# A two-layer hybrid backbone step on one core: substitution columns dealt in turn, R1 made by TensorE, a 3 + 2 split of token tiles behind a norm, and four tiles for the first merge's gates

## The chip, the cores and the metric

The program runs on one core of one Trainium2 chip. The time is that of one execution on the device in microseconds. TensorE (PE) multiplies, VectorE (DVE), ScalarE (ACT) and GpSimd (POOL) work on elements, SyncE (SP) issues all DMAs. TensorE's full clock is 2.4 GHz, its low one 1.2 GHz.

## The reference

Two layers (DEPTH 2) act on 128 context tokens and 512 latent tokens of width 1024, all in float32. A layer projects the modulated input once into three branches (gated MLP over chunks, grouped attention, a bidirectional delta rule), projects each branch back, gates and sums the three, projects the sum, adds it to the input and normalises; then comes an MLP with squared ReLU of width 4096 and a second norm.

```python
f = _token_shift(concat([rkv, lora[:, :, d]]), mu, reverse=(d == 1))       # d = 0, 1
S = S * w_t[:, :, None, :] + sa[..., None] * b_t[:, :, None, :] + v_t[..., None] * k_t[:, :, None, :]
p = einsum('bljc,jcd->bljd', branches, P['w_branch'][l])
mixed = sum(gates * p, axis=2) @ P['w_out'][l]
x = _layer_norm(ALPHA * x + g1 * mixed, ln1_g, ln1_b)
f = square(relu(h @ P['w_up'][l])) @ P['w_down'][l]
x = _layer_norm(ALPHA * x + g2 * f, ln2_g, ln2_b)
```

## The kernel before, in words

The 640 tokens lie as five tiles of 128 (tile 0 is context). Every large product takes weights and inputs split into a high part and a rest (`whalf`, `split`: ScalarE copies the high part, VectorE subtracts, L241 and L242), and three matmuls for each. The instructions are written out in an order by hand; a planner then puts them on the engines' queues by that order as priority, as their inputs and buffers become free in its own timeline, so later work (the gate projections `gl`, say) fills TensorE in earlier stages.

**The delta rule.** There are eight units a layer (four head pairs, two directions). A unit has seven steps: 1, load r, k and the decay; 2, scale them and store the key norms (`ssd`); 3, products G of 64-token chunks and their transposes `bk`; 4, the solve; 5, transposes `av`, products `w`, and the load of the solved blocks into `Ga`; 6, products `z1`, `z2`, `tx`, `xp`; 7, a scan over the chunks in eight steps (`st`). `rwkv` (L647) interleaves them: for each unit u step 3 of u, step 1 of u+1, the solve of u, steps 6 and 7 of u-1, step 5 of u, step 2 of u+1, with pieces of projections and attention between.

**The solve (step 4).** For 40 blocks of 32x32 (two halves, 20 chunk-heads) T = inverse of a unit triangular matrix is made by substitution. The blocks are read from DRAM (`ad` to `ab`) three times, on 120 partitions: group g holds columns 11g to 11g+10 of each block. Each of the 31 steps multiplies (L861) and adds (L862) on all 11 columns of every group; unit 3 of each layer does so on GpSimd, the others on VectorE. Then a copy `Tr` (L864), three writes of `td`, three writes of a transposed `tr`; `td` is loaded into the diagonal blocks of `Ga`, `tr` into `R1`, the operand of z1.

**PSUM.** Pool B has two buffers and serves step 2 (`ss`, `bo`), 3, 5 and 6 of all units. Pool A has two pairs for the projections.

**Behind a norm.** `res_end` normalises tile by tile, transposes a tile and writes its high part and rest into hT (`put_hT`; its last split is L392). `fm_blocks` then does its first three blocks in two parts of the token columns: all three on columns below `CUT` (256: two tiles), then all three on the rest. That is so at three places: the first MLP chunk of either layer, and the second layer's first projection.

**The last of four MLP chunks** starts with rows for the gate and norm, and for each token tile two GpSimd multiplies (L1207) and two VectorE adds of ALPHA x (L1208), ahead of the chunk's first block.

**Merge A** takes, for each of eight output blocks, the gate from DRAM into a tile `f` (two buffers, shared with the gate projections and the branch loads), multiplies the block by it (L1037) and stores the product (`part`). Merge B and C follow; C loads its branches into e0 to e2. e0 to e4 are otherwise a unit's inputs, one buffer each.

Of the kernel before, what the change touches and what calls it, by code (L numbers as in the profile page):

```python
# [40 lines left out]
RS, AFW = (), 512  # L41
FILL, FILLA, NG, CUT = 1, 4, 24, 256
K13 = ["e0", "e1", "e2", "e3", "e4", "w", "w", "Ld", "ec", "bon", "bon", "Y0", "Y1"]
# [15 lines left out]
class Net:  # L59
# [654 lines left out]
    def unit(self, l, hp, d):  # L714
# [134 lines left out]
        nc.vector.tensor_tensor(out=Am, in0=Am, in1=n2.unsqueeze(1).to_broadcast([3 * NB, 32, 32]), op=ALU.mult)  # L849
        nc.gpsimd.memset(raw[:, 0:1024:33], 1.0)  # L850
        T = self.S([3 * NB, CG, 32], "T", bufs=2)
# [5 lines left out]
        for q in range(31):  # L857
            i, js = (q, slice(q + 1, 32)) if d == 0 else (31 - q, slice(0, 31 - q))
            sh = [3 * NB, CG, 31 - q]
            p = Pm[:, :, 0:31 - q]  # L860
            eng.tensor_tensor(out=p, in0=T[:, :, i:i + 1].to_broadcast(sh), in1=Am[:, i, js].unsqueeze(1).to_broadcast(sh), op=ALU.mult)  # L861
            eng.tensor_tensor(out=T[:, :, js], in0=T[:, :, js], in1=p, op=ALU.add)  # L862
        Tr = self.S([3 * NB, 32, CG], "Pm", bufs=2)
        nc.vector.tensor_copy(Tr, T.rearrange("p c i -> p i c"))  # L864
        td = self.dram.tile([2, NI, 32, 32], F32, name=self.nm("td"))
        tr = self.dram.tile([NI, 32, 32], F32, name=self.nm("tr"))
        tdv = td.rearrange("f i s t -> (f i) s t")
        for g in range(3):
            w = min(CG, 32 - CG * g)
            self.load(tdv[:, CG * g:CG * g + w, :], T[g * NB:g * NB + NB, 0:w, :])  # L870
            p0 = g * NB + d * NI
            self.load(tr[:, :, CG * g:CG * g + w], Tr[p0:p0 + NI, :, 0:w])
        yield
# [35 lines left out]
        Z = R1  # L909
        self.load(R1[fa], tr.rearrange("i t s -> t i s"))  # L910
        ps = self.B("z1")
# [114 lines left out]
    def gated(self, l, j, dp, xs):  # L1026

        nc, a = self.nc, self.a
        wb = self.wsplit(a["wbr"][l, j, dp].rearrange("p t k c -> p (t k c)"))
        gs = []  # L1030
        for dt in range(2):
            g = self.K("f" if j == 0 else "fQ"[dt] if j == 1 else "PQ"[dt])
            self.load(g[:, 0:NTOK], self.gate[l][8 * j + 2 * dp + dt])
            ps = self.A("br", None if j else 0)
            self.mm_fm(ps, wb[dt:dt + 1], xs)
            for o, p in self.ev(ps, g):
                nc.vector.scalar_tensor_tensor(o, o, 1.0, p, ALU.add, ALU.mult)  # L1037
            gs.append(g[:, 0:NTOK])
        return gs
# [152 lines left out]
    def mlp(self, l, hT, xsrc, xdst, nxt, side):  # L1192
# [4 lines left out]
        for pc in range(NPC):  # L1197
# [5 lines left out]
            if pc == NPC - 1:  # L1203
                self.res_rows(r, xsrc)
                for t in range(NT):
                    for x, yh, h in self.res_x(r, t):
                        nc.gpsimd.tensor_tensor(out=yh, in0=yh, in1=r.g[0 if t == 0 else 1][h], op=ALU.mult)  # L1207
                        nc.vector.scalar_tensor_tensor(yh, x, ALPHA, yh, ALU.mult, ALU.add)  # L1208
            ups = self.fm_blocks([a["wup"][l, 8 * pc + i].rearrange("p k c -> p (k c)") for i in range(8)], hT, pc == 0)
            for i, ps in enumerate(ups):  # L1210
# [5 lines left out]
                self.split(f, hi, lo)  # L1216
                xs.append((hi, lo))
                self.steps(side, 3)
            if pc == NPC - 1:
# [231 lines left out]
def shape_constants():  # L1451
# [15 lines left out]
    for g in range(3):  # L1467
        for j in range(CG):
            if CG * g + j < 32:
                e[g, :, j, CG * g + j] = 1  # L1470
    o["E"] = e.reshape(6 * NI, CG, 32)
# [40 lines left out]
```

## Time and profile before

| | us |
|---|---|
| three runs | 2956.73, 2965.16, 2951.77 (median 2956.73) |
| profiled execution | 2957.33 |
| its span, first to last instruction | 2955.5 |
| TensorE's mean granted clock | 0.961 of full |

In the rows, PE is a TensorE matmul and PEld its weight load. "out<-in" are the program's names of tiles; "128x512 f32" is partitions x elements. A group's row ends with the mean ns of one instruction, the idle time of the engine ahead of the group, and what ended it. Matmuls overlap, so the ns of one matmul is longer than the distance to the next.

### The profile page before, as it was taken

Reading aid. Unit: us, or ns where it says so; the run is one execution under the profiler, and the core shown is the slowest. Engines: PE = TensorE matmul, PEld = TensorE weight load, DVE = VectorE, ACT = ScalarE, POOL = GpSimd, SP = SyncE. Lnnn points to the kernel's source line nnn. Section 1 sums busy time; section 2 is a strip of 40 time slices with the busy share of each in tenths; the row PEclk is TensorE's granted clock in tenths of the full one; section 3 lists DMA queues with packets and bytes.
Section 4 is the critical chain, followed back from the end, with each engine's and each line's share of the span. In section 5 each row is a group of like instructions: output and inputs, shape, how many; then the busy total and the mean of one; then the engine's idle time right before and its main releaser. Section 6 shows DMA issues by size and latency. Waiting matters only on the chain.

```text
span 2955.5 us, 56368 instructions
## 1 busy us (share of the span) xinstructions
PE 2769.2 (94%) x21248; PEld 2518.1 (85%) x21248; DVE 1957.2 (66%) x3824; ACT 1365.6 (46%) x3206; POOL 681.6 (23%) x869
## 2 busy tenths in 40 slices
PE   7989989999979899999989899899999898999998
PEld 5979877787869889999989788787877798999998
DVE  5686877877777776777464878877676566223346
ACT  3445665565653433232444456654655434342332
POOL 4241271312333400002040312813121014000021
PEclk8989989999989999999999899899999999999999
DMA  8534323343476254545235333333433652222242
GB/s 265 182 113 117 103 84 92 99 112 91 125 241 211 98 150 152 153 147 183 94 107 161 110 112 100 102 86 91 111 93 111 214 172 76 76 76 72 76 134 84
DMA packets 326647, 367.88 MB, mean 124 GB/s; under 512 B 157599, under 2 KB 179607, under 8 KB 326375
## 3 DMA queue, kind: packets, MB, share of 16 engines
q1 hardware_dynamic: 326375, 364.28, 40.9%
q8 instruction: 167, 2.74, 0.4%
q14 instruction: 105, 0.86, 0.1%
HBM read 301.59 MB, written 62.59 MB: 123 GB/s over the span
## 4 chain that ended last, share of the span: by engine, by line
PE 62%; DVE 16%; DMA 10%; ACT 5%; issue 4%; SPq 2%; POOL 1%; DVEq 0%; ACTq 0%; POOLq 0%
PE fm L163 17%; PE tm L207 17%; PE gl L163 7%; PE br L163 4%; PE tm L233 2%; SPq L125 2%; PE uA L163 2%; PE g L820 2%; DVE T L862 2%; DVE Pm L861 2%; PE xp L939 1%; DVE lo L242 1%; PE st L974 1%; DMA ab<-ad 1%; PE ada L319 1%
## 5 line engine op out<-in xcount | busy, mean ns | idle before, releaser
L242 DVE TENSOR_TENSOR lo<-raw,hi 128x512 fp32r<-128x512 f32 x514 | 381.9, 745 | 402.2 <-ACT hi L241 391.2
L163 PE MATMUL fm<-h,hi 128*128 128x320 f32 (+1 forms) x2720 | 616.5, 316 | 14.8 <-ACT h L391 10.2
L241 ACT ACTIVATE hi<-raw 128x512 fp32r<-128x512 f32 x514 | 323.0, 630 | 593.6 <-PE tm L207 320.2
L163 PEld LDWEIGHTS fm<-h,hi 128*128 128x128 f32 x2720 | 464.5, 192 | 33.0 <-ACT h L391 11.5
L163 PE MATMUL fm<-h,lo 128*128 128x320 f32 (+2 forms) x1360 | 421.7, 316 | 8.4 <-DVE lo L242 8.3
L163 PE MATMUL gl<-h,hi 128*128 128x320 f32 x1536 | 375.6, 322 | 0.0
L163 PEld LDWEIGHTS gl<-h,hi 128*128 128x128 f32 x1536 | 263.4, 191 | 19.5 <-issue 10.7
L163 PEld LDWEIGHTS fm<-h,lo 128*128 128x128 f32 x1360 | 259.8, 192 | 12.9 <-DVE lo L242 9.6
L163 PE MATMUL gl<-h,lo 128*128 128x320 f32 x768 | 248.2, 324 | 1.9 <-DVE lo L242 1.9
L861 DVE TENSOR_TENSOR Pm<-T,ab 120x341 f32<-120x341 f32 (+30 forms) x434 | 171.7, 396 | 9.0
L862 DVE TENSOR_TENSOR T<-T,Pm 120x341 f32<-120x341 f32 (+30 forms) x434 | 170.3, 392 | 9.5
L312 DVE SCALAR_TENSOR_TENSOR acc<-P,c_sg,acc 128x512 f32<-128x512 f32 x196 | 143.3, 771 | 45.6 <-DMA P<-in_wada_dram 44.9
L1207 POOL TENSOR_TENSOR X<-X,e 128x512 f32<-128x512 f32 x8 | 11.6, 1456 | 682.5 <-DMA e<-modd 354.6
L207 PE MATMUL tm<-hi,h 128*128 128x256 f32 x800 | 158.7, 292 | 0.0
L163 PEld LDWEIGHTS gl<-h,lo 128*128 128x128 f32 x768 | 146.8, 191 | 9.0 <-issue 2.5
L163 PE MATMUL br<-h,hi 128*128 128x320 f32 x512 | 123.1, 329 | 23.1 <-DVE f L1037 11.8
L207 PEld LDWEIGHTS tm<-hi,h 128*128 128x128 f32 x800 | 129.2, 195 | 4.8 <-issue 1.6
L207 PE MATMUL tm<-hi,L 128*128 128x256 f32 x720 | 131.8, 283 | 0.0
L978 ACT ACTIVATE q1k<-st,edge 64x64 f32<-64x64 f32 x320 | 98.2, 307 | 66.1 <-PE st L974 60.5
L537 POOL TENSOR_TENSOR P<-P,Q 128x512 f32<-128x512 f32 x64 | 83.6, 1307 | 154.6 <-ACT Q L532 53.2
L207 PE MATMUL tm<-lo,h 128*128 128x256 f32 x400 | 115.9, 291 | 3.1 <-DVE lo L242 3.1
L163 PEld LDWEIGHTS br<-h,hi 128*128 128x128 f32 x512 | 89.4, 198 | 29.6 <-DVE f L1037 9.4
(560 smaller groups left out, 6879.2 us busy)
## 6 DMA issues: line engine op xcount, KB each, us to landing
raw<-in_win_f_dram SPq DMA_DIRECT2D x172, 256.0 KB
raw<-in_wup_dram SPq DMA_DIRECT2D x128, 256.0 KB
raw<-in_wdn_dram SPq DMA_DIRECT2D x128, 256.0 KB
P<-in_wada_dram SPq DMA_DIRECT2D x114, 256.0 KB
w<-rk SPq DMA_DIRECT2D x48, 321.5 KB
gate<-f SPq DMA_DIRECT2D x48, 320.0 KB
raw<-in_wbr_dram SPq DMA_DIRECT2D x48, 256.0 KB
Ld<-rk SPq DMA_DIRECT2D x64, 160.0 KB
```

Source lines behind the costliest of these rows:

```text
L125: self.nc.sync.dma_start(out=out, in_=in_)
L163: nc.tensor.matmul(ps.at(h), w[:, c], ps.of(h, x), start=(k == 0 and p == 0), stop=(k == n - 1 and p == 2))
L207: nc.tensor.matmul(out[t], x[:, ts], w[:, c], start=(k == 0 and p == 0 and (alone or t < 2)), stop=(k == n - 1 and p == 2 and (alone or t ...
L233: nc.tensor.matmul(o, x[:, ts], w[:, c], start=(k == 0 and p == 0), stop=(k == n - 1 and p == 2))
L241: self.nc.scalar.activation(hi, x, AF.Copy)
L242: self.nc.vector.tensor_sub(lo, x, hi.bitcast(F32))
L312: nc.vector.scalar_tensor_tensor(acc[:, s], w, cs[:, k, s:s + 1], acc[:, s], ALU.mult, ALU.add)
L537: nc.gpsimd.tensor_tensor(out=den, in0=den, in1=PT, op=ALU.add)
L820: nc.tensor.matmul(pg[h][:, 128 * j:128 * j + 128], BK[pr, c0 + j].rearrange("p s t -> p (s t)"), RAV[pr, c0 + j, 0:2, :].rearrange("p s t ...
L861: eng.tensor_tensor(out=p, in0=T[:, :, i:i + 1].to_broadcast(sh), in1=Am[:, i, js].unsqueeze(1).to_broadcast(sh), op=ALU.mult)
L862: eng.tensor_tensor(out=T[:, :, js], in0=T[:, :, js], in1=p, op=ALU.add)
L978: nc.scalar.activation(St[kr, s, h, :], p4[kr, s, h, :], AF.Copy, scale=edge[kr, cc:cc + 1])
```

## The change

Columns are dealt: group g now holds columns g, g+3, g+6 and so on of each block, and step q works only on the columns that can be non-zero by then (q//3 + 1 of 11). The memset of the diagonal, the copy `Tr` and the DRAM tensor `tr` are gone; `td` is written column by column. R1 is made in step 6 by matmuls of `Ga`'s diagonal blocks with the identity, into two tiles of pool B, and a ScalarE copy of each. CUT is 384 (three tiles, then two). Merge A's gates go to e0 to e3 in turn. In the last MLP chunk tile i's multiplies and adds stand behind block i.

```diff
--- before.py
+++ after.py
@@ -39,7 +39,7 @@
 EARLY = 2
 ADAR, FIRST = (12, 3), 5
 RS, AFW = (), 512
-FILL, FILLA, NG, CUT = 1, 4, 24, 256
+FILL, FILLA, NG, CUT = 1, 4, 24, 384
 K13 = ["e0", "e1", "e2", "e3", "e4", "w", "w", "Ld", "ec", "bon", "bon", "Y0", "Y1"]
 RAWB, WB = 3, 3
 
@@ -847,7 +847,6 @@
         nc.vector.reciprocal(n2, n2)
         Am = raw.rearrange("p (s t) -> p s t", s=32)
         nc.vector.tensor_tensor(out=Am, in0=Am, in1=n2.unsqueeze(1).to_broadcast([3 * NB, 32, 32]), op=ALU.mult)
-        nc.gpsimd.memset(raw[:, 0:1024:33], 1.0)
         T = self.S([3 * NB, CG, 32], "T", bufs=2)
         Pm = self.S([3 * NB, CG, 32], "Pm", bufs=2)
         nc.vector.tensor_tensor(out=T, in0=c["E"], in1=n2.unsqueeze(1).to_broadcast([3 * NB, CG, 32]), op=ALU.mult)
@@ -856,20 +855,15 @@
         eng = nc.gpsimd if on_pool else nc.vector
         for q in range(31):
             i, js = (q, slice(q + 1, 32)) if d == 0 else (31 - q, slice(0, 31 - q))
-            sh = [3 * NB, CG, 31 - q]
-            p = Pm[:, :, 0:31 - q]
-            eng.tensor_tensor(out=p, in0=T[:, :, i:i + 1].to_broadcast(sh), in1=Am[:, i, js].unsqueeze(1).to_broadcast(sh), op=ALU.mult)
-            eng.tensor_tensor(out=T[:, :, js], in0=T[:, :, js], in1=p, op=ALU.add)
-        Tr = self.S([3 * NB, 32, CG], "Pm", bufs=2)
-        nc.vector.tensor_copy(Tr, T.rearrange("p c i -> p i c"))
+            cs = slice(0, q // 3 + 1) if d == 0 else slice(max(0, (31 - q) // 3), CG)
+            sh = [3 * NB, cs.stop - cs.start, 31 - q]
+            p = Pm[:, cs, 0:31 - q]
+            eng.tensor_tensor(out=p, in0=T[:, cs, i:i + 1].to_broadcast(sh), in1=Am[:, i, js].unsqueeze(1).to_broadcast(sh), op=ALU.mult)
+            eng.tensor_tensor(out=T[:, cs, js], in0=T[:, cs, js], in1=p, op=ALU.add)
         td = self.dram.tile([2, NI, 32, 32], F32, name=self.nm("td"))
-        tr = self.dram.tile([NI, 32, 32], F32, name=self.nm("tr"))
         tdv = td.rearrange("f i s t -> (f i) s t")
         for g in range(3):
-            w = min(CG, 32 - CG * g)
-            self.load(tdv[:, CG * g:CG * g + w, :], T[g * NB:g * NB + NB, 0:w, :])
-            p0 = g * NB + d * NI
-            self.load(tr[:, :, CG * g:CG * g + w], Tr[p0:p0 + NI, :, 0:w])
+            self.load(tdv[:, g::3, :], T[g * NB:g * NB + NB, 0:(34 - g) // 3, :])
         yield
         X = self.units["X"] = self.units.get("X") or self.big1("X", [128, NI, 128])
         X4 = X.rearrange("p (c h) n -> p c h n", h=2)
@@ -907,7 +901,12 @@
         ra, rb_ = ([slice(64 * h + o, 64 * h + o + 32) for h in range(2)] for o in (a_, b_))
         R1 = self.big1("R1", [128, NI * 32]).rearrange("p (i t) -> p i t", t=32)
         Z = R1
-        self.load(R1[fa], tr.rearrange("i t s -> t i s"))
+
+        for h in range(2):
+            ps = self.B("r1")
+            for c_ in range(NCH):
+                nc.tensor.matmul(ps[fa, 32 * c_:32 * c_ + 32], Ga[ra[h], c_, h, fa], c["ident"][ra[h], ra[h]], start=True, stop=True)
+            nc.scalar.activation(R1[fa].rearrange("p (c h) t -> p c h t", h=2)[:, :, h, :], ps[fa, 0:32 * NCH].rearrange("p (c t) -> p c t", t=32), AF.Copy)
         ps = self.B("z1")
         for c_ in range(NCH):
             for h in range(2):
@@ -1029,7 +1028,7 @@
         wb = self.wsplit(a["wbr"][l, j, dp].rearrange("p t k c -> p (t k c)"))
         gs = []
         for dt in range(2):
-            g = self.K("f" if j == 0 else "fQ"[dt] if j == 1 else "PQ"[dt])
+            g = self.K(f"e{2 * (dp % 2) + dt}" if j == 0 else "fQ"[dt] if j == 1 else "PQ"[dt])
             self.load(g[:, 0:NTOK], self.gate[l][8 * j + 2 * dp + dt])
             ps = self.A("br", None if j else 0)
             self.mm_fm(ps, wb[dt:dt + 1], xs)
@@ -1202,10 +1201,6 @@
             xs = []
             if pc == NPC - 1:
                 self.res_rows(r, xsrc)
-                for t in range(NT):
-                    for x, yh, h in self.res_x(r, t):
-                        nc.gpsimd.tensor_tensor(out=yh, in0=yh, in1=r.g[0 if t == 0 else 1][h], op=ALU.mult)
-                        nc.vector.scalar_tensor_tensor(yh, x, ALPHA, yh, ALU.mult, ALU.add)
             ups = self.fm_blocks([a["wup"][l, 8 * pc + i].rearrange("p k c -> p (k c)") for i in range(8)], hT, pc == 0)
             for i, ps in enumerate(ups):
                 f = self.K("f")
@@ -1215,6 +1210,10 @@
                 hi, lo = bufs[2 * i], bufs[2 * i + 1]
                 self.split(f, hi, lo)
                 xs.append((hi, lo))
+                if pc == NPC - 1 and i < NT:
+                    for x, yh, h in self.res_x(r, i):
+                        nc.gpsimd.tensor_tensor(out=yh, in0=yh, in1=r.g[0 if i == 0 else 1][h], op=ALU.mult)
+                        nc.vector.scalar_tensor_tensor(yh, x, ALPHA, yh, ALU.mult, ALU.add)
                 self.steps(side, 3)
             if pc == NPC - 1:
                 for _ in side:
@@ -1466,8 +1465,8 @@
     e = np.zeros((3, 2 * NI, CG, 32), f4)
     for g in range(3):
         for j in range(CG):
-            if CG * g + j < 32:
-                e[g, :, j, CG * g + j] = 1
+            if 3 * j + g < 32:
+                e[g, :, j, 3 * j + g] = 1
     o["E"] = e.reshape(6 * NI, CG, 32)
     inv = f4(10000.0) ** (-np.arange(0, 32, 2, dtype=f4) / f4(32))
     cos, sin = np.ones((NTOK, 64), f4), np.zeros((NTOK, 64), f4)
```

## Rows read from the trace of the kernel before

**Rows 1.** The page, part 1: busy us, share of the span, number of instructions.

```profile
PE 2769.2 (94%) x21248; PEld 2518.1 (85%) x21248; DVE 1957.2 (66%) x3824; ACT 1365.6 (46%) x3206; POOL 681.6 (23%) x869
```

**Rows 2.** Stretches of the span: stretch, its us, busy us of each engine, PEclk, DMA share, GB/s.

```profile
143.00:450.00 307.00, 272.17 (x2293) 244.81 (x2292) 240.77 (x558) 173.57 (x471) 123.90 (x195) 0.91 0.37 103
450.00:822.00 372.00, 362.40 (x2938) 297.09 (x2937) 284.12 (x593) 216.41 (x587) 88.97 (x96) 0.99 0.37 106
822.00:900.00 78.00, 59.08 (x376) 51.09 (x374) 57.88 (x82) 38.96 (x89) 32.22 (x22) 0.89 0.81 260
983.00:1045.00 62.00, 52.93 (x365) 50.37 (x364) 42.74 (x79) 30.36 (x55) 31.62 (x30) 0.89 0.28 94
2301.00:2370.00 69.00, 57.89 (x414) 53.00 (x414) 36.71 (x70) 28.63 (x80) 10.14 (x6) 0.95 0.73 231
```

**Rows 3.** Stretches of the first solve and of GpSimd's solve, same columns.

```profile
143.00:201.00 58.00, 47.99 (x317) 42.65 (x315) 53.66 (x117) 26.75 (x55) 24.19 (x24) 0.82 0.34 100
373.00:435.00 62.00, 49.96 (x389) 43.22 (x390) 49.73 (x100) 40.26 (x118) 55.28 (x80) 0.85 0.27 85
```

**Rows 4.** Groups of instructions of the solve, by line and engine.

```profile
L861 DVE TENSOR_TENSOR Pm<-T,ab 120x341 f32<-120x341 f32 (+30 forms) x434 | 171.7, 396 | 9.0
L862 DVE TENSOR_TENSOR T<-T,Pm 120x341 f32<-120x341 f32 (+30 forms) x434 | 170.3, 392 | 9.5
L864 DVE COPY Pm<-T 120x352 f32<-120x352 f32 x16 | 8.5, 529 | 0.2
L862 POOL TENSOR_TENSOR T<-T,Pm 120x341 f32<-120x341 f32 (+30 forms) x62 | 42.7, 689 | 4.2
L861 POOL TENSOR_TENSOR Pm<-T,ab 120x341 f32<-120x341 f32 (+30 forms) x62 | 40.1, 647 | 4.3
```

**Rows 5.** Adds of the solve on VectorE by shape, 14 of each.

```profile
L862 DVE TENSOR_TENSOR T<-T,Pm 120x330 f32<-120x330 f32 x14 | 7.0, 500 | 0.3
L862 DVE TENSOR_TENSOR T<-T,Pm 120x11 f32<-120x11 f32 x14 | 2.5, 179 | 0.3
```

**Rows 6.** z1 as a group, then z1, its copies and z2 of one unit in time.

```profile
L914 PE MATMUL z<-R,L 32*32 32x32 f32 x640 | 16.6, 193 | 1.4 <-DMA R<-tr 1.4
641.21 0.25 PE L914 MATMUL z<-R,L 32*32 32x32 f32 x4
643.86 0.88 ACT L916 ACTIVATE R<-z 32x320 f32<-32x320 f32 x2 [0.71 <-PE z L914]
647.16 0.24 PE L921 MATMUL z<-L,R 32*32 32x32 f32 x2
```

**Rows 7.** Transfers on the chain of waits near one solve: start us, us until landed.

```profile
635.17 2.27 DMA ad<-L
778.67 2.67 DMA td<-T
783.35 2.15 DMA R<-tr
```

**Rows 8.** The first norm: two stretches, then the last splits of third and fifth tile.

```profile
1020.00:1029.00 9.00, 2.42 (x12) 1.44 (x10) 7.34 (x11) 5.01 (x10) 8.67 (x8) 0.69 0.23 89
1034.00:1045.00 11.00, 11.00 (x66) 11.00 (x65) 4.76 (x8) 6.04 (x11) 0.00 (x0) 1.00 0.42 121
1013.75 0.68 DVE L392 TENSOR_TENSOR h<-f,h 128x512 fp32r<-128x512 f32 x1
1029.37 1.92 DVE L392 TENSOR_TENSOR h<-f,h 128x512 fp32r<-128x512 f32 x2
```

**Rows 9.** The last MLP chunk: a GpSimd multiply; TensorE's wait for a split.

```profile
1386.90 1.73 POOL L1207 TENSOR_TENSOR F<-F,e 128x512 f32<-128x512 f32 x1
1403.93 0.63 PE L163 MATMUL fm<-h,lo 128*128 128x320 f32 x1 [4.14 <-DVE lo L242]
```

**Rows 10.** Waits in the whole span, longest sums: who for whom, us, times, longest.

```profile
DVE f L1037 <- DMA f<-gate: 19.1, 8, 5.9
PE br L163 <- DVE f L1037: 11.8, 7, 4.5
```

## Prediction

> **What bounds the kernel now.** I read the page first. TensorE is busy 2769.2 of 2955.5 us; VectorE has 66%, ScalarE 46% [rows 1]. So the first question about any edit off TensorE is which TensorE idle time it can remove: there are 186 us of it in all. The view of the stretches says where. In the first layer's recurrence up to 450 us TensorE is idle for 307 - 272.17 = 34.8 us and its granted clock is 0.91; at 1.2 GHz instead of 2.4 for 18% of the time, the 272 busy us hold some 0.09 x 272 = 24 us more of loss. From 450 to 822 us, with gate projections as filler, only 9.6 us are idle at clock 0.99. The merge has 18.9 us idle in the first layer and 11.1 in the second, the norm 9.1 [rows 2]. The recurrent stage of the second layer (1626 to 2301 us) and the two other norms (1490 and 2446 us) repeat these patterns, as does the last chunk at 2816 us. Third, what the solve does to its stretch: while it runs VectorE is busy 53.66 of 58 us in the first unit; in the unit on GpSimd, GpSimd is busy 55.28 of 62 us and VectorE still 49.73; these two stretches, at clocks 0.82 and 0.85, hold 10.0 and 12.0 us of the 34.8 idle [rows 3].
>
> **The solve (dealt columns).** Each of 31 steps has a multiply and an add over 11 x (31-q) elements. 434 of each on VectorE (14 solves) take 171.7 and 170.3 us, so 24.4 us a solve; GpSimd's two take 82.8 us, 41.4 each [rows 4]. An add of 330 elements takes 500 ns, one of 11 takes 179 ns: 1.0 ns an element, and 168 ns that don't shrink [rows 5]. The old elements per pass are 11 x 496 = 5456. With columns dealt in threes only q//3+1 of them are non-zero at step q, so the new sum of (q//3+1) x (31-q) is 1991. A new solve is 62 x 0.168 + 2 x 1.991 = 14.4 us: 10.0 us less, 140 us over 14 solves. Most is saved early in a solve, where 341 elements become 31. GpSimd's solve by the same ratio falls from 41.4 to 24.4, 17 us each. The copy Tr goes too, 8.5 us [rows 4]. Work off TensorE thus falls by 140 + 34 + 8 = 182 us; the question is how much TensorE waits for it.
>
> In the early part of a layer the two stretches of rows 3 lose 10.0 + 12.0 us idle and 0.18 x 48 + 0.15 x 50 = 16 us of clock, 38 in all. The first solve (58 us) loses 14 us of its own work, the GpSimd one (62 us) 17, so each stretch shrinks by about a quarter, and I take a quarter of its loss, 10 us, and 5 us for the other 21 us of loss in that part (two more solves in it): 15 a layer, 30 for both. Bounds: 0 (TensorE has filler for all of it) and 59 a layer (all idle and clock loss there). In the late part only 9.6 us are idle; I take 2 a layer, 4 in all, between 0 and 9.6 a layer. What is late next there is TensorE's own filler.
>
> **R1 through TensorE.** Before, R1 came by way of DRAM (three writes of tr, one load). Now, in step 6, twice ten 32x32 products with the identity and two ScalarE copies stand ahead of z1, in two more tiles of the two-buffer PSUM pool B. No row shows them; nearest are z1's own: 16.6 us for 16 units, 1.04 us of TensorE a unit, and two copies in 0.88 us [rows 6]. So 16.6 us more TensorE work and 14 us of ScalarE, which is 46% busy. The wait is the dearer part: the order z1, two copies, z2 took from 641.21 to 647.16 us in one unit, so a step of this kind costs 5.95 us in line [rows 6]. Behind it on TensorE stand z1 and the filler, and for z1 wait z2, tx, xp and the scan. The bounds are -2 us a unit (the load of R1 alone takes 2.15 us to land, [rows 7], and is gone) and +5.95: -32 to +95 us. I take the TensorE work with less than half of it hidden, +10 us: near z1's own rows rather than the step in line, because the filler's matmuls are there to run while the copies are awaited.
>
> **The round trip of T.** td is now written in runs of 32 floats (128 bytes) instead of 1408. The write of ad has runs of 128 bytes already and took 2.27 us to land, td 2.67 [rows 7]; I take 0. SP loses three issues a unit and the load of R1. The Trainium skill ("DMA: Bandwidth & Descriptors", Specifications) gives 512 bytes as the least for line rate, with a read-modify-write below it. By that rule the td write would be slower; the two rows don't show it, and the sum goes by the rows. The GpSimd memset of the diagonal, one of two waits ahead of a solve's first step, goes; I count 0, between 0 and the few tenths that such an instruction takes.
>
> **The norm (CUT 384).** Before, 72 matmuls over 256 columns start when two token tiles are normed, and 72 over 384 when all five are. Between them, from 1020 to 1029 us, TensorE is busy 2.42 of 9 us at clock 0.69; then it goes without a break, 66 matmuls in 11 us, so 0.167 us for one of 384 columns and 0.111 for one of 256 [rows 8]. Now the first 72 have 384 columns and need the third tile, whose last split ends at 1013.75 + 0.68 = 1014.4. They take 12.0 us, to 1026.4, still ahead of the last tile's split, which ends at 1029.37 + 1.92 = 1031.3 [rows 8]: the wait for the third tile costs nothing as long as that holds. The columns are the same in sum; what stands behind the last tile falls from 72 x 0.167 = 12.0 us to 8.0. I take 4.3 us, a little over these 4.0, because the clock is low where that part starts and it now holds shorter matmuls; three times, 13. Bounds: 0 (the third tile slips behind the weight splits on VectorE) and 6.6 (all the idle time of 1020 to 1029).
>
> **The last MLP chunk.** Ten GpSimd multiplies of up to 1.73 us and ten VectorE adds stood ahead of the first weight splits; TensorE then waits 4.14 us for a split [rows 9]. Spread behind the first five blocks of eight they have 48 matmuls of 320 columns each to hide in, 48 x 0.139 = 6.7 us by the rate of rows 8. SP's loads of x move with them, behind the weight loads of each block. I take 3 us a layer, 6; bounds 0 and 4.1 a layer.
>
> **Gates of merge A.** The load of a gate waited for one of two f tiles, whose store had to land: VectorE waited 19.1 us for those loads in the second layer, TensorE 11.8 us for VectorE behind it, both layers [rows 10]. Four tiles let the loads go ahead. They are the delta rule's e0 to e3, free since the last unit's second step; merge C's loads of e0 to e2 now wait for merge A's last stores, with merge B between. I take 9 of the 11.8; bounds 0 and 30 (all idle of both merges).
>
> **Sum.** -30 - 4 + 10 - 13 - 6 - 9 = -52 us. The profiled execution took 2957.33 us (1.8 outside its span), the median of the runs is 2956.73, 0.6 less. 2957.3 - 52 = 2905.
>
> **Rivals.** (B) *VectorE sets the recurrent stage.* For it: VectorE is 92% busy in a solve's stretch [rows 3]. Against: TensorE has 9.6 us idle in 372. If half of the 182 us comes off the path, and the other edits give 28: 2957 - 91 - 28 = 2838.
> (C) *The solve was hidden.* TensorE's filler covers what VectorE saves, and only R1's 17 us of work show: 2957 + 17 - 28 = 2946, no change.
> (D) *Slower: the R1 step lies in line.* Place: ahead of z1, in pool B; if its two buffers go round in program order, R1 can't take one before the next unit's step 3 has let go, though its input landed long before. Price 5.95 us a unit, 95 for sixteen; with the solve hidden as in C, 2957 + 95 - 28 = 3024, and 2977 if half of the units pay. It makes the kernel slower from the fifth paying unit on (28 / 5.95). Against: the filler, and that the scan of the previous unit runs beside.
> (E) *Short runs cost the td write another 2.67 us a unit,* a second landing, as if read first: +43, 2948. Rows 7 speak against. The page named above is its source.
>
> **Chances.** Forecast 0.57, B 0.14, C 0.17, D 0.10, E 0.02. A measurement of this kernel can tell 0.5%, 15 us, from no change. The forecast's own range is 2875 to 2935. The range of all runs from 2855 (a tenth, most of B, below) to 2955 (D above). Faster: 0.56 of the forecast, B, 0.04 of C: 0.74. Slower: 0.09 of D. The same: 0.17.
>
> **What would show it.** L861 and L862 on VectorE sum to 200 us for 14 solves instead of 342; above 230 the slope is wrong. TensorE idle in the early part falls from 35 to some 25 us a layer, with the clock up to 0.93 or more; if it stays, C. If z1 starts 4 us or more after the next unit's bk has ended, and the time from one solve's start to the next grows, D; if that distance falls by 5 us or more a unit in the late part, B. After a norm TensorE goes without a break from the last tile's split and ends some 4 us sooner; if the 384-column half starts later than 4 us after the third tile's split, that edit gives nothing. The 4.14 us wait for a split goes. In merge A the gate loads are issued ahead of the matmuls, and VectorE no longer waits for them. A time above 2942 or under 2875 would make the forecast's sizes wrong.

## The result, and the profile after

The changed kernel took 2924.88 us (median of 4 runs, 2923.61 to 2929.32), the kernel before 2954.31 beside it: ratio 0.9898, 95% interval 0.9876 to 0.9919. A second measurement (below) gave 0.9864 (0.9841 to 0.9886). So it is faster, by 1% or 29 us where 52 were forecast. The profiled execution has a span of 2921.8 us, 33.7 less than that of [rows 1].

Part 1 of the page after, and the line of its part 4 that gives the chain's shares by engine:

```profile
PE 2788.8 (95%) x21888; PEld 2530.8 (87%) x21888; DVE 1839.9 (63%) x3808; ACT 1378.9 (47%) x3238; POOL 657.4 (23%) x853
...
PE 74%; DVE 9%; DMA 7%; ACT 6%; issue 3%; SPq 1%; POOL 1%; DVEq 0%; ACTq 0%; POOLq 0%
```

TensorE is busy 19.6 us longer than in [rows 1] (its 640 new matmuls), in a span 33.7 us shorter: 53 us of its idle time are gone. VectorE lost 117 us and GpSimd 24.

The solve's groups on VectorE and on GpSimd, which answer to [rows 4], and three shapes of its add, which answer to [rows 5]:

```profile
L861 DVE TENSOR_TENSOR Pm<-T,ab 120x72 f32<-120x72 f32 (+24 forms) x434 | 124.4, 287 | 11.1
...
L862 DVE TENSOR_TENSOR T<-T,Pm 120x72 f32<-120x72 f32 (+24 forms) x434 | 116.8, 269 | 10.8
```

```profile
L861 POOL TENSOR_TENSOR Pm<-T,ab 120x72 f32<-120x72 f32 (+23 forms) x62 | 29.3, 473 | 9.5 <-DVE ab L849 5.2
L862 POOL TENSOR_TENSOR T<-T,Pm 120x72 f32<-120x72 f32 (+23 forms) x62 | 28.5, 459 | 4.5
```

```profile
L862 DVE TENSOR_TENSOR T<-T,Pm 120x84 f32<-120x84 f32 x36 | 9.8, 271 | 0.9
...
L862 DVE TENSOR_TENSOR T<-T,Pm 120x31 f32<-120x31 f32 x14 | 2.5, 181 | 0.2
L862 DVE TENSOR_TENSOR T<-T,Pm 120x11 f32<-120x11 f32 x14 | 4.5, 324 | 0.3
```

14 solves on VectorE take 241.2 us, 17.2 each, where 14.4 were forecast. The sum, 241.2, lies above the 230 that the prediction named as the sign of a wrong slope. But an add of 31 elements costs what the slope says (168 + 31 ns; measured 181); one of 11 elements, 179 ns in [rows 5], now has a mean of 324, which no slope explains (see the last section).

Stretches of the recurrent stage, from the start and from the end of layer 2's first long matmul stretch to the last gl matmul of each layer, with the part of layer 1 from 140 to 450 us; columns as in [rows 2]. First the kernel before, then the one after:

```profile
140.00:450.00 310.00, 275.17 (x2318) 247.81 (x2317) 241.93 (x558) 173.96 (x472) 123.90 (x195) 0.91 0.37 105
0.00:822.80 822.80, 761.51 (x6000) 648.29 (x6001) 605.94 (x1265) 451.46 (x1182) 260.87 (x380) 0.95 0.43 126
1636.40:2301.10 664.70, 621.47 (x5121) 533.47 (x5119) 501.89 (x1112) 379.45 (x1034) 202.38 (x283) 0.95 0.37 102
```

```profile
140.00:450.00 310.00, 288.44 (x2482) 259.75 (x2481) 214.35 (x557) 179.32 (x486) 111.53 (x191) 0.91 0.37 109
0.00:816.20 816.20, 768.59 (x6189) 651.29 (x6191) 551.51 (x1242) 449.56 (x1161) 254.41 (x374) 0.95 0.42 127
1619.70:2274.40 654.70, 630.97 (x5474) 539.68 (x5475) 443.59 (x1096) 389.36 (x1067) 189.28 (x276) 0.96 0.35 102
```

Span minus busy is TensorE's idle time: 61.3 to 47.6 us in layer 1, 43.2 to 23.7 in layer 2, and 34.8 to 21.6 from 140 to 450 us, where some 25 was forecast. But the busy time grew by 7.1 and 9.5, and the clock in that part stayed at 0.91, where 0.93 was forecast.

The same landmarks on TensorE cut every trace of this study into stages, in us: the last gl, the last br (the branch products of a merge), and behind a norm the first tm (products with tokens as rows, here the next stage's). Norm 1 and 3 hold the out-projection of 60 us ahead of them; MLP 1 ends ahead of norm 2; "rest" is layer 2's MLP to the end. 37.9 us between norm 2 and layer 2's recurrent stage, alike in all, are left out.

```
run             recur.1 merge1 norm1  MLP1  norm2 recur.2 merge2 norm3  rest
before            822.8  124.1 137.9  429.4  84.3  664.8  108.6  133.3  412.5
after             816.2  122.6 131.6  430.8  80.7  654.7  103.9  131.2  412.3
after again       818.1  121.1 131.4  430.9  80.7  658.9  105.3  128.5  412.7
a1 full solve     823.5  129.7 131.3  431.5  79.5  667.9  107.0  127.0  413.2
a2 R1 by DRAM     822.3  121.8 130.2  431.9  82.7  672.2  108.4  131.2  412.3
a3 CUT 256        817.8  124.3 139.5  429.6  83.9  666.5  108.5  132.6  414.1
a4 gates in f     819.9  124.0 130.1  430.9  83.1  662.3  113.8  127.8  414.4
a5 chunk back     819.8  125.7 131.5  433.0  81.0  658.0  103.2  128.3  413.1
a6 recurr. only   811.4  127.7 136.7  428.8  84.6  669.9  107.2  133.0  412.5
b1 cut, gates     824.7  117.0 129.3  431.3  80.3  674.7  107.1  127.3  411.3
n1 order only     815.3  128.5 131.0  430.7  79.0  665.4  110.1  128.8  412.8
c1 no GpSimd      821.1  129.5 133.2  429.8  80.2  655.0  109.0  127.3  414.3
c2 R1 one tile    818.7  130.9 131.4  431.7  81.7  651.9  106.4  128.9  410.1
d1 no solve       798.1  131.8 133.3  430.4  80.2  636.9  111.0  128.2  409.6
```

One row is one execution. How far to trust a cell is seen in the seven runs whose instructions on TensorE stand in the same order up to layer 1's last gl, but for one pair at the very start (after, again, a3, a4, a5, a6, n1): 811.4 to 819.9, mean 816.9. This scatter goes with the granted clock: the stage has 0.96 in a6, the shortest, and 0.94 in a4, the longest; why, no run shows. Before and b1, which share the older order, have 822.8 and 824.7. Where one price is given for several runs below, it is the difference of a kernel's ratio from 0.9881, the mean of after's two, times 2955 us.

### The profile page after: what moved, and what is told of

Its sections match the earlier page's. It is cut to its first block, busy times and chain, and to the rows that moved or that the text cites. A ratio compares the mean times of both kernels' runs of the same rounds, so it can differ in the third digit from the quotient of the medians.

```text
span 2921.8 us, 57547 instructions
## 1 busy us (share of the span) xinstructions
PE 2788.8 (95%) x21888; PEld 2530.8 (87%) x21888; DVE 1839.9 (63%) x3808; ACT 1378.9 (47%) x3238; POOL 657.4 (23%) x853
## 4 chain that ended last, share of the span: by engine, by line
PE 74%; DVE 9%; DMA 7%; ACT 6%; issue 3%; SPq 1%; POOL 1%; DVEq 0%; ACTq 0%; POOLq 0%
PE fm L163 20%; PE tm L207 18%; PE gl L163 10%; PE br L163 4%; PE g L820 2%; PE tm L233 2%; PE xp L938 2%; PE st L973 2%; PE o L535 1%; PE uA L163 1%; PE tx L927 1%; PE at L506 1%; DVE lo L242 1%; PE ada L319 1%; ACT q1k L977 1%
## 5 line engine op out<-in xcount | busy, mean ns | idle before, releaser
L242 DVE TENSOR_TENSOR lo<-raw,hi 128x512 fp32r<-128x512 f32 x514 | 376.0, 734 | 409.6 <-ACT hi L241 404.2
L207 PE MATMUL tm<-hi,L 128*128 128x256 f32 x720 | 131.8, 283 | 0.0
L861 DVE TENSOR_TENSOR Pm<-T,ab 120x72 f32<-120x72 f32 (+24 forms) x434 | 124.4, 287 | 11.1
L862 DVE TENSOR_TENSOR T<-T,Pm 120x72 f32<-120x72 f32 (+24 forms) x434 | 116.8, 269 | 10.8
L207 PEld LDWEIGHTS tm<-hi,L 128*128 128x128 f32 x720 | 113.1, 192 | 1.7 <-issue 0.9
```

The source lines that it names most:

```text
L207: nc.tensor.matmul(out[t], x[:, ts], w[:, c], start=(k == 0 and p == 0 and (alone or t < 2)), stop=(k == n - 1 and p == 2 and (alone or t ...
L242: self.nc.vector.tensor_sub(lo, x, hi.bitcast(F32))
L861: eng.tensor_tensor(out=p, in0=T[:, cs, i:i + 1].to_broadcast(sh), in1=Am[:, i, js].unsqueeze(1).to_broadcast(sh), op=ALU.mult)
L862: eng.tensor_tensor(out=T[:, cs, js], in0=T[:, cs, js], in1=p, op=ALU.add)
```

## The experiments

The first theory: the gain comes from the norms, the first merge and a little of the recurrent stage, and most of the solve's saving has slack. What spoke for it was the load of the solved blocks into Ga: before, it followed the solve's end; after, in five of the eight units of layer 1, half of it is issued 22 to 26 us later than the other half, behind the w matmuls that read the blocks it overwrites.

**a1: each step of the solve over all 11 slots.**

```diff
-            cs = slice(0, q // 3 + 1) if d == 0 else slice(max(0, (31 - q) // 3), CG)
+            cs = slice(0, CG)
```

> The kernel after, but with each step of the solve over all 11 column slots again (the dealing of the columns, R1 through TensorE and the rest stay). Each solve should be near 24 us on its engine again instead of 17. Theory (most of the saved solve time has slack: before the change the solved blocks were waited for, after it the load into Ga waits for the w matmuls that read the old blocks): 2924.9 + 3 to 12, that is 2928 to 2937, ratio to before about 0.992 to 0.994. Rival (the shorter solve is the gain, 15 us a layer as forecast): 2924.9 + 30 = 2955, ratio 1.00.

2950.1 us, ratio 0.9965 (0.9951 to 0.9978). That is 25 us, nearer the rival's 30 than the theory's 3 to 12. The solve on VectorE is back at (179.7 + 170.7) / 14 = 25.0 us, and layer 1's idle time at 61 us:

```profile
L861 DVE TENSOR_TENSOR Pm<-T,ab 120x341 f32<-120x341 f32 (+30 forms) x434 | 179.7, 414 | 9.3
...
L862 DVE TENSOR_TENSOR T<-T,Pm 120x341 f32<-120x341 f32 (+30 forms) x434 | 170.7, 393 | 9.7
```

```profile
0.00:823.50 823.50, 762.35 (x6188) 646.37 (x6189) 608.29 (x1241) 448.45 (x1157) 261.59 (x369) 0.96 0.42 125
```

Beside after the stage has 13.5 us more idle time, but its matmuls, as many as after's, are busy 6.2 us less (762.35 against 768.59), at a granted clock of 0.96 against 0.95. So of the idle time that the shorter solve takes away, the stage keeps only about half; what sets this difference in the clock, no run shows.

**a2: R1 through DRAM again** (in layout of the dealt columns, 33 wide).

```diff
+        Tr = self.S([3 * NB, 32, CG], "Pm", bufs=2)
+        nc.vector.tensor_copy(Tr, T.rearrange("p c i -> p i c"))
...
+            self.load(tr[:, :, CG * g:CG * g + CG], Tr[p0:p0 + NI])
...
-        for h in range(2):
-            ps = self.B("r1")
...
+        self.load(R1[fa].rearrange("p i j g -> p i g j"), tr.rearrange("i t (g j) -> t i g j", g=3))
```

> The kernel after, but R1 comes again as a transposed copy on VectorE, written to DRAM and loaded by a DMA, without the 20 matmuls a unit through pool B. Theory (the step stands in line between the load of Ga and z1, two evictions and a turn of the two buffers of pool B, and costs about what was forecast): faster than after by about 10 us, 2915, ratio 0.9865. Rival 1 (R1 through TensorE costs nothing, or the DMA load and the VectorE copy of 11 x 32 elements cost as much): 2922 to 2928, ratio 0.989 to 0.991. Rival 2 (the removed copy and loads were a gain): 2935, ratio 0.9935.

2947.7, ratio 0.9948 (0.9931 to 0.9966): slower than after by some 20 us. The theory, that R1 through TensorE costs about 10, fell, and rival 2 is nearest. Layer 1 shows how:

```profile
0.00:822.30 822.30, 764.22 (x5976) 652.43 (x5976) 557.63 (x1264) 451.24 (x1173) 252.28 (x374) 0.94 0.44 127
```

TensorE is busy 4.4 us less than after, as it should be, and idle 10.5 us more. (Its order on TensorE is another one as well, in both layers.)

**a3: the norm's first block over 256 columns.**

```diff
-FILL, FILLA, NG, CUT = 1, 4, 24, 384
+FILL, FILLA, NG, CUT = 1, 4, 24, 256
```

> The kernel after with the first block behind a norm over 256 of the 640 columns again. Theory (three norms gave 6.4, 3.7 and 2.1 us between the last column before and the first long stretch after each norm, by the landmarks of the two traces): 2924.9 + 12 = 2937, ratio 0.994. Rival (what a norm gave is given back before the next one, or belongs to something else): 2925, ratio 0.990.

2951.0, ratio 0.9968 (0.9956 to 0.9980): 26 us worse than after, where 12 were expected. Of these the three norms explain 7.9 + 3.2 + 1.4 to 4.1 us, and MLP 1 gives 1.2 back. Another 8 to 12 stand in layer 2's recurrent stage, whose code is untouched. The hole behind the norm is there again: a stretch of a3, then the two of after that answer to it, and after's last split:

```profile
1015.00:1025.00 10.00, 2.59 (x16) 1.79 (x15) 8.34 (x13) 5.49 (x11) 9.93 (x8) 0.77 0.22 84
```

```profile
1012.00:1022.00 10.00, 9.98 (x64) 9.59 (x62) 4.01 (x7) 4.47 (x10) 6.42 (x5) 1.00 0.08 28
1022.00:1032.00 10.00, 8.06 (x65) 7.86 (x66) 6.32 (x11) 6.39 (x13) 5.35 (x4) 1.00 0.49 169
```

```profile
1023.39 2.81 DVE L392 TENSOR_TENSOR h<-f,h 128x512 fp32r<-128x512 f32 x2
```

TensorE, busy 2.6 of 10 us in a3 while it waits for the last tiles, at a granted clock of 0.77 (a mean over its two levels, 1.2 and 2.4 GHz), is busy 18 of 20 us in after, all at the upper level; the last split ends at 1026.2, and between the matmuls of the blocks (`fm`) lie holes of 0.6, 1.4 and 0.5 us instead of one of 8.8.

**a4: the first merge's gates in the two f tiles.**

```diff
-            g = self.K(f"e{2 * (dp % 2) + dt}" if j == 0 else "fQ"[dt] if j == 1 else "PQ"[dt])
+            g = self.K("f" if j == 0 else "fQ"[dt] if j == 1 else "PQ"[dt])
```

> The kernel after with the first merge's gates in the two tiles f again. Theory (the merge stretch of layer 1 gave 1.5 us and that of layer 2 gave 4.7 by the landmarks): 2924.9 + 6 = 2931, ratio 0.992. Rival (9 us as forecast): 2934, ratio 0.993; rival 2 (the next wait took its place): 2925, ratio 0.990.

2939.2, ratio 0.9928 (0.9910 to 0.9946), 14 us worse than after. The wait for the gate loads is back in a4 (first fence; columns: who for whom, us, times, longest) and after has none. But TensorE's wait for VectorE in the merges is 7.3 us in a4 and still 2.7 + 2.2 + 1.9 = 6.8 in after (second):

```profile
DVE f L1036 <- DMA f<-gate: 10.4, 5, 4.4
PE br L163 <- DVE f L1036: 7.3, 6, 2.3
```

```profile
PE br L163 <- DVE Q L1036: 2.7, 2, 1.8
...
PE br L163 <- DVE f L1036: 2.2, 2, 1.5
PE br L163 <- DVE e L1036: 1.9, 3, 1.0
```

The merge of layer 1 is 1 to 3 us longer than in the two after runs, that of layer 2 some 9, and layer 2's recurrent stage is again 3 to 8 us longer without a reason in its code.

So the four undoing runs cost 25 + 20 + 26 + 14 = 85 us beside a change worth 29 to 40. They can't all be prices. The second theory: after any edit the planner sets the instructions of layer 2's recurrent stage in another order, and the order of the kernel after happens to be a good one. The next runs did parts alone.

**b1: the kernel before with CUT 384 and the e tiles alone** (the two edits of a3 and a4 in the other direction).

```diff
-FILL, FILLA, NG, CUT = 1, 4, 24, 256
+FILL, FILLA, NG, CUT = 1, 4, 24, 384
...
-            g = self.K("f" if j == 0 else
+            g = self.K(f"e{2 * (dp % 2) + dt}" if j == 0 else
```

> The kernel before with two edits alone: three token tiles first behind a norm, and the first merge's gates in four tiles. Theory (the norms give 12 us and the merge 6 by the landmarks of the two traces, and nothing that leaves the recurrent stage alone can move it): 2954.3 - 18 = 2936, ratio 0.994. Rival (undoing these two cost 20.7 and 9 us in the runs so far, and these are their prices): 2954 - 30 = 2925, ratio 0.990, as good as the whole change. Rival 2 (the planner lays layer 2's recurrent stage out anew after every edit ahead of it, and that is where 10 us of each of the undoing runs went): the stage from layer 2's first matmul block behind the norm to its last gl column differs from before's by 5 to 15 us though its code is the same.

2938.0, ratio 0.9914 (0.9890 to 0.9938): about 25 us, though layer 2's recurrent stage, with the code of before, took 674.7 instead of 664.8. Rival 2 of the expectation came true as well. (Its one profile is 14.5 us below that of before, not 25: the profiled execution of before, 2957.3 us, is among the short ones of a kernel whose runs beside b1 went from 2953.3 to 2971.8.)

**a6: the recurrent stage's edits alone** (after, with the edits of a3, a4 and a5 undone).

```diff
-FILL, FILLA, NG, CUT = 1, 4, 24, 384
+FILL, FILLA, NG, CUT = 1, 4, 24, 256
...
-            g = self.K(f"e{2 * (dp % 2) + dt}" if j == 0 else
+            g = self.K("f" if j == 0 else
```

> The kernel before with the recurrent stage's edits alone (dealt columns, R1 through TensorE); norms, merge and last chunk as before. Theory (landmarks: layer 1's recurrent stage gives 7 us, layer 2's 10): 2954.3 - 17 = 2937, ratio 0.994. Rival (undoing the solve cost 20 us and undoing R1 cost 15, so together they give 35): 2920, ratio 0.988. Rival 2 (layer 2's part is the planner's luck): -7, 2947, ratio 0.9975.

2957.5, ratio 0.9983 (0.9967 to 0.9999): 5 us. Layer 1's stage has gained, layer 2's has not (669.9). Rival 2 is the nearest.

**a5: the last chunk's multiplies ahead of the block loop again** alone.

```diff
                 self.res_rows(r, xsrc)
+                for t in range(NT):
+                    for x, yh, h in self.res_x(r, t):
...
-                if pc == NPC - 1 and i < NT:
-                    for x, yh, h in self.res_x(r, i):
```

> The kernel after with the last chunk's multiplies back ahead of the block loop. Theory (the last chunk took 65.1 us before and 65.3 after in layer 1, 60.7 and 60.6 in layer 2: nothing gained): 2925, ratio 0.990, or up to 12 us more if layer 2's recurrent stage comes out in another order. Rival (3 us a layer as forecast): +6, 2931, ratio 0.992, with each last chunk 3 us longer.

2930.1, ratio 0.9887 (0.9865 to 0.9908), against 0.9864 for after beside it: 7 us, but the intervals overlap, so the times alone don't tell the edit's worth from nothing. Its TensorE order in layer 2 is that of after, entry for entry, and its stage there is, too: 658.0. What the edit did not do is plain. The wait in front of the chunk that it was to remove is the same, in after and in a5 as in [rows 9]:

```profile
1367.82 1.29 POOL L1215 TENSOR_TENSOR X<-X,e 128x512 f32<-128x512 f32 x1 [340.46 <-DMA e<-modd]
...
1385.37 1.73 POOL L1215 TENSOR_TENSOR y<-y,e 128x512 f32<-128x512 f32 x1
1390.84 0.63 PE L163 MATMUL fm<-h,lo 128*128 128x320 f32 x1 [4.14 <-DVE lo L242]
```

```profile
1399.57 0.63 PE L163 MATMUL fm<-h,lo 128*128 128x320 f32 x1 [4.26 <-DVE lo L242]
```

The first fence is after's, the second a5's. In the program the multiplies now stand behind the blocks; on GpSimd all ten of layer 1 still run closely behind one another, the first 23.0 us ahead of that matmul and the last ending at 1387.1. In the trace of before the first stood at 1380.92, 23.0 us ahead of the matmul of [rows 9] as well. The last chunk's up-projection takes 65.6 and 60.9 us in the two layers in after and 65.8 and 61.6 in a5, so no worth of the edit shows.

**The kernel after, again.**

> The kernel after, unchanged, beside the others of this call, as their mark. Theory: ratio 0.9898 again (0.9876 to 0.9919). Rival: nearer to 0.993, and then a part of what each undoing run showed (sum 65 us) is no price of its edit.

2923.2, ratio 0.9864 (0.9841 to 0.9886). The result holds, and is no worse than the first time, so it is the undoing runs whose sum is too large.

**n1: an edit with no work in it.** In layer 1's first merge the four e tiles are taken in reverse.

```diff
-            g = self.K(f"e{2 * (dp % 2) + dt}" if j == 0 else
+            g = self.K(f"e{2 * (dp % 2) + dt if l else 3 - 2 * (dp % 2) - dt}" if j == 0 else
```

> The kernel after with an edit without any work in it: in layer 1's first merge the four gate tiles are taken in reverse. TensorE's order is the same up to layer 1's last gl column; behind it the planner lays layer 2's recurrent stage out in another order, as in the runs that undid the norm's cut and the gates. Theory (part of what the undoing runs showed is that order and no price of the edit): layer 1's recurrent stage within 2 us of after's 816 to 820, layer 2's 5 to 12 us longer than after's 655 to 659, so the time 5 to 12 us above after, ratio 0.990 to 0.992. Rival (order costs nothing, the undoing runs showed prices): layer 2's stage 655 to 660, ratio 0.9864 to 0.9898 as after.

2935.7, ratio 0.9919 (0.9893 to 0.9946). All six of its runs (2933.1 to 2942.3) lie above all nine of after (2918.1 to 2929.3). By the ratio that is 11 us above after. Layer 1's stage: 815.3; layer 2's: 665.4, the theory's numbers. Not all of it lies there: the merges took 128.5 us (the one with the edit; 121.1 to 127.7 in the other six of its order) and 110.1 (103.2 to 105.3 in the order of after). Stretches of layer 2's recurrent stage in after again, a5 (the good order), a3 and n1:

```profile
1620.20:2279.10 658.90, 635.42 (x5474) 543.93 (x5475) 442.85 (x1096) 389.52 (x1067) 189.06 (x276) 0.95 0.35 101
```

```profile
1628.80:2286.80 658.00, 633.87 (x5474) 542.49 (x5475) 443.21 (x1097) 389.39 (x1067) 189.44 (x276) 0.95 0.36 101
```

```profile
1633.00:2299.40 666.40, 632.43 (x5410) 539.85 (x5409) 444.97 (x1078) 382.94 (x1040) 192.86 (x275) 0.95 0.35 100
```

```profile
1622.50:2287.80 665.30, 630.73 (x5295) 536.41 (x5293) 444.49 (x1079) 378.13 (x1020) 188.26 (x272) 0.95 0.35 101
```

Idle 23.5 and 24.1 us in the good order, 34.0 and 34.6 in these two others (29.5 and 29.3 in a4 and a6). Where the orders part can be counted in the traces: between the bk transposes of the fourth and the fifth unit of layer 2 stand 48 gl matmuls in after, after again and a5, and the step takes 77 us in each; 127, 126 and 128 in a3, a4 and n1, and it takes 93, 93 and 102. The count marks an order, it doesn't explain the time: c2 below has 127 there and takes 83 us, and its stage, 651.9, is the shortest but d1's.

**c1: the fourth unit's solve on VectorE too.**

```diff
-POOLT = (3,)
+POOLT = ()
```

> The kernel after with the fourth unit's solve on VectorE too, not on GpSimd: 17 to 30 us in place of 46. Theory (in that unit the load into Ga follows the end of the solve at once, so here the solve is still waited for): TensorE idle up to 450 us from 21.6 to some 16 us in layer 1, 5 us a layer, 2915, ratio 0.985. Rival (VectorE, already busy 212 of 302 us there, holds up the evictions of that stretch by the 17 us that it gains): the same or up to 8 us slower, ratio 0.988 to 0.992.

2934.0, ratio 0.9906 (0.9878 to 0.9933). No gain: idle up to 450 us is 24.6 us (21.6 to 26.9 in the seven runs), layer 1's stage 821.1. The rival, that VectorE has to hold what GpSimd gives up, is nearer; with layer 2's order changed too, no more can be read from it.

**c2: both halves of R1 in one tile of pool B.**

```diff
-        for h in range(2):
-            ps = self.B("r1")
...
+        ps = self.B("r1")
+        for c_ in range(NCH):
+            for h, fo in enumerate((fa, fb)):
+                nc.tensor.matmul(ps[fo, 32 * c_:32 * c_ + 32], Ga[ra[h], c_, h, fa], c["ident"][ra[h], ra[h]], start=True, stop=True)
```

> The kernel after with both halves of R1 in one tile of pool B (the second half on the other 32 partitions) instead of two. One turn of the pool's two buffers less a unit. Theory (the R1 step in line sets the last units of a layer, bk to bk 98 us against 84 before, but there TensorE has filler and only 6.6 us idle, so little comes of it): units six and seven of layer 1 some 3 us shorter, layer 1's recurrent stage 0 to 3 us shorter than 816 to 820, time -6 to 0 against after. Rival (step in line sets the end): -3 us a unit, 40 us in all, 2885, ratio 0.975.

2931.4, ratio 0.9897 (0.9868 to 0.9926). The turn of the pool doesn't set the end: the sixth and seventh units stand 96 and 99 us apart from the next (99 and 98 in after), and the stage took 818.7.

**d1: no solve at all** (the loop of 31 steps runs zero times, so T is only its starting value: this leaves out part of the computation).

```diff
-        for q in range(31):
+        for q in range(0):
```

> The kernel after with all 31 steps of the solve left out of every unit (T is only its scaled starting value, so what the kernel gives isn't the reference): 17 us of VectorE less a unit, 46 us of GpSimd in the fourth. It tells what is still to be had from the solve. Theory (in five of eight units the load into Ga now waits for w and not for the solve, and the second half of a layer has 6.6 us idle; only units two and four and the first still wait): layer 1's recurrent stage 809 to 814 instead of 815 to 820, TensorE idle up to 450 us from 21.6 to 14 or 17; time 2905 to 2918, ratio 0.982 to 0.987. Rival (the solve is on the path throughout: 7 us a solve gave 6 us a layer, so 17 more give 15): layer 1's stage 800 to 804, time 2890, ratio 0.977. Rival 2 (nothing of it is left on the path): layer 1's stage 815 to 820, ratio 0.987 to 0.992.

2901.2, ratio 0.9807 (0.9783 to 0.9831), 22 to 24 us below after. Layer 1's stage is 798.1, 18.8 below the mean of the seven; layer 2's is 636.9.

```profile
140.00:450.00 310.00, 291.92 (x2580) 263.91 (x2579) 178.91 (x381) 182.87 (x492) 87.49 (x132) 0.93 0.39 112
0.00:798.10 798.10, 758.76 (x6110) 644.41 (x6110) 442.92 (x809) 444.36 (x1146) 229.43 (x310) 0.96 0.43 130
1611.80:2248.70 636.90, 616.14 (x5265) 525.59 (x5263) 342.60 (x677) 375.14 (x1015) 165.68 (x210) 0.97 0.36 104
```

My theory of slack falls here: layer 1's stage gives more than even the rival said. The time, 2901, lies between the two (2905 to 2918, and 2890), for the merges take part of it back: 131.8 and 111.0 us, some 10 and 6 more than the mean of after's two. That the load waits for w is true and was misread. My reading, which no run separated from the wait for the solve's result: the solve costs TensorE time on VectorE too, and with it gone, what stands behind it in VectorE's queue comes earlier.

No version was faster than the kernel after, save d1, which doesn't compute the solve.

## Why the prediction was right, and where its sizes were off

The direction and the likeliest case held, with 29 of the 52 us. That the time lay within the forecast's own range, up to 2935, was in part luck: some 9 of the 29 us came from an order that no term held (last step below), and without them it would have been about 2934. By its steps:

- **The solve's own time** (14.4 us forecast, 17.2 measured). The slope was right, its use was not. I took 14.4 from fixed cost and slope alone and subtracted it from a measured 24.4; the same formula gives 62 x 0.168 + 2 x 5.456 = 21.3 for the old solve. Both kernels have some 3 us a solve on top that don't shrink with the elements. The saving is 7.2, not 10.0, and GpSimd's solve went from 41.4 to 28.9, not 24.4. The first solve, for which 14 us less were taken, went from 28.8 to 17.4.
- **What it brings the stage** (15 + 2 us a layer forecast). Layer 1: -6.8 us (mean of two against mean of seven), R1's edit included. The quarter of the stretches' loss that I took was about right for idle time (34.8 to 21.6 us, and 24.1 on the mean of the seven; forecast 25), but the 5 us a layer for the clock did not come (0.91 before, 0.91 on the mean of the seven). Per us of VectorE solve a unit, the stage gives (823.5 - 816.9) / 7.8 = 0.85 us a layer from a1 and 18.8 / 17.2 = 1.1 from d1; the forecast had 17 / 10 = 1.7. This is the term that was mis-sized most: the idle time went as forecast, but the gain in clock did not come, and the longer busy time took back half. Layer 2's -10.1 us are mostly order (below): against the four other orders the two older runs (mean 669.8) are only 3.7 us longer.
- **R1 through TensorE** (+10). Its 640 matmuls are busy 26.9 us by their own row and its copies 13.4 us; TensorE's busy time grew by 7.1 + 9.5 = 16.6 in the two stages, all of the work priced. But the way by DRAM came out dearer (a2: 20 us by time, layer 1's stage 5.4 us longer than the mean of the seven, 2.4 longer than the longest of them), so the sign of this term was probably wrong. It isn't shown apart from the order, which a2 changes too, and what of the DRAM way would cost so much stays open; z1 itself waited only 1.4 us for that load in [rows 6].

```profile
L908 PE MATMUL r<-c_ident,L 32*32 32x32 f32 x640 | 26.9, 195 | 1.1 <-issue 1.1
...
L909 ACT ACTIVATE R<-r 32x320 f32<-32x320 f32 x32 | 13.4, 425 | 11.0 <-PE r L908 10.2
```

- **The round trip of T** (0): the one td write on the chain of after landed in 2.02 us, those on the chain of before in 2.67 [rows 7] to 4.09. Rival E, 43 us for a second landing, is out. The Trainium skill's 512 bytes ("DMA: Bandwidth & Descriptors", Specifications) are not to be seen in this landing.
- **The norm** (-13). Kernels with 256 (before, a3, a6) against those with 384: 138.0 to 131.3, 84.3 to 80.8, 133.0 to 128.6 on the mean, 14.6 together, less 1.9 that the following MLP of layer 1 takes longer. 12.7: the sum that was right, and the largest gain that can be shown. Singly the norms gave 6.7, 3.4 and 4.4, where 4.3 was taken for each.
- **The last chunk** (-6): its mechanism did not happen, and the 4.14 us wait is still there. The step failed where I took the place in the program for the place in time. The planner had GpSimd do the ten multiplies at the same distance from the wait, wherever the lines stood. And it is beside these multiplies that VectorE is slow: in after a split takes 1.78 us while they run and 0.68 behind them (the last section shows the same in the solve). How much of the 4.14 us is theirs, no run shows.

```profile
1380.76 1.78 DVE L242 TENSOR_TENSOR lo<-raw,hi 128x512 fp32r<-128x512 f32 x1
...
1390.10 0.68 DVE L242 TENSOR_TENSOR lo<-raw,hi 128x512 fp32r<-128x512 f32 x1
```

- **Gates of the first merge** (-9): the wait for the gate loads went, as forecast, and 11.8 us of TensorE's wait became 2.7 + 2.2 + 1.9 = 6.8. So 5 of the 11.8, and the two merges are 1.5 and 4.7 us shorter between the two traces. But a4, which undoes this edit alone, has 7.3 us of that wait, and both merges scatter by more than this: layer 1's took 121.1 to 128.5 us with the four tiles and 124.0 and 127.7 without, in the seven runs with one order ahead of it, and layer 2's depends on the order as well (103 to 114 us). A gain of this edit is not shown beyond 1 us of TensorE's wait. The step that failed took that wait to be the loads': with them awaited (a4, 10.4 us on VectorE) TensorE waits 7.3 us, without (after) 6.8.
- **What no term had: the order.** Layer 2's recurrent stage has 654.7 to 658.9 us in the order of the kernel after, and 662.3 to 669.9 with the same recurrent code in four other orders (a3, a4, a6, n1); the older code had 664.8 and 674.7. Some 9 of the 29 us (657.2 against 666.0 on the mean, a5 counted with after) are the planner's order, which no edit aimed at. After's order is not the only good one: c1 and c2, in two more orders and with edits of their own, have 655.0 and 651.9.

The stages of before less those of after: 6.6 + 1.5 + 6.3 - 1.4 + 3.6 + 10.1 + 4.7 + 2.1 + 0.2 = 33.7, the difference of the spans.

Of the rivals, B is out (the late part did not fall by 5 us a unit). C said that the solve is hidden; d1 refutes it. D's sign did appear in layer 1: the last two steps from bk to bk went from 96 and 84 us to 99 and 98. But they lie beside gate projections with 6.6 us idle, and c2 takes a turn out for nothing: it has no price.

## What to carry to other kernels

Price a shrinking chain of small instructions by applying the same formula to both sides: what a measured duration holds on top of it stays. Where a planner orders the instructions, an edit in one place moves the order elsewhere; before a price is read from undoing one part, compare the orders, and run one edit that does no work to learn what an order is worth (here some 9 us, nearly a third of the result). A line moved in the program is moved in time only if the engine's order changes with it.

## What the runs showed of the hardware that I had not expected

A VectorE step of the solve that begins while a long GpSimd instruction with inputs runs is held, with few exceptions, until that one ends; beside a GpSimd memset, which has none, it isn't. In after, at 448.7 and at 172 us (start, us, engine, line):

```profile
448.70 1.63 POOL L748 TENSOR_TENSOR e<-Ld,e 64x640 fp32r<-64x640 f32 x1 [9.14 <-ACT e L747]
448.83 1.55 DVE L861 TENSOR_TENSOR Pm<-T,ab 120x31 f32<-120x31 f32 x1
450.41 0.19 DVE L862 TENSOR_TENSOR T<-T,Pm 120x31 f32<-120x31 f32 x1
450.64 0.19 DVE L861 TENSOR_TENSOR Pm<-T,ab 120x30 f32<-120x30 f32 x1
```

```profile
172.04 1.16 POOL L893 MEMSET L<- 64x1280 f32 x1
172.47 0.21 DVE L862 TENSOR_TENSOR T<-T,Pm 120x63 f32<-120x63 f32 x1
172.72 0.22 DVE L861 TENSOR_TENSOR Pm<-T,ab 120x54 f32<-120x54 f32 x1
```

The same 31 elements cost 1.55 us beside GpSimd's subtraction and 0.19 behind it. Set against GpSimd's instructions, the 868 VectorE steps of the trace fall apart: 698 that overlap none have a mean of 225 ns and none over 268. Of the 170 that overlap one, 92 lie beside a memset alone (mean 236) and 24 began ahead of the GpSimd instruction (218), none over 268 either. Of 52 that began while a long one with inputs (over 0.6 us) ran, 49 ended 34 to 145 ns behind its end, with a mean of 1143 and up to 1612; 3 were not held, nor were the last 2, beside short ones. The 170 have a mean of 494, so 170 x 0.269 = 46 us, 3.3 a solve, nearly all of it from the 49; before it was 191 x 0.234 = 45 us. This is the part that did not shrink. The Trainium skill ("SBUF — State Buffer", Who interferes with whom) says that a VectorE instruction with two SBUF inputs contends with a GpSimd instruction that reads SBUF, not with one that only writes it, and that the contention is an exclusive lock. The rows above agree, for the case that VectorE comes second; whether GpSimd is held when it comes second, no row here shows.
